# A two-layer RWKV-7/attention backbone on one core: running decays by a sum of exponents, token mixing in one VectorE pass, both heads' removal keys in one instruction

## The chip, the cores and the metric

The kernel runs on one core of one Trainium2 chip. The metric is device microseconds of one execution. The engines are named as the profile names them: PE (TensorE matmul) with PEld (its weight loads), DVE (VectorE), ACT (ScalarE), POOL (GpSimd) and SP (SyncE, which issues most DMAs). Each engine works through its own list of instructions in order; semaphores tie the lists together.

## The reference

Two layers work on a context stream and a latent stream of 256 tokens each, width 1024. A layer makes one modulated input, projects it with one weight matrix `w_in`, and feeds three mixers: latent attention, a short convolution, and a bidirectional recurrence. Their outputs are gated, merged and projected, and a SwiGLU feed-forward follows. The change lies in the recurrence alone. Cut to what it touches:

```python
def rwkv_features(part, mu, ...):
    up = _pad_seq(part)
    part = part + (0.5 * (up[:, :-2] + up[:, 2:]) - part) * mu         # token mixing
    r, k, v, wd, ad, gd = _split(part, ...)
    w_log = -softplus(-(w0 + tanh(wd) @ w_up)) - 0.5
    decay = exp(-exp(w_log))                                            # per token and channel
    a = sigmoid(a0 + ad @ a_up)
    kk = k * k_k / norm_per_head                                        # removal key
    k_dir = k * (1 + (a - 1) * k_a)

def step(S, inp):                                                       # once forward, once backward
    r, w, k, v, kk, a = inp
    S = S * w - (S @ kk) (kk * a)^T + v k^T
    return S, S @ r
```

With `exp(w_log) = sigmoid(x) * exp(-0.5)` and the sigmoid written as `0.5 + 0.5 tanh(x/2)`, one token's decay is `exp(-0.5 CEXP (tanh + 1))`, where `CEXP = exp(-0.5)`. The kernel runs the recurrence in chunks of 64 tokens. A chunk needs the product `P` of the decays from the chunk's start to each token, and its inverse `Pi`.

## The kernel before

Products of weights and activations run as three float32r matmuls (`mm3`, L199 to L201): every piece of weights is fetched by SP, copied to its high part on ACT (L188) and its low part formed on DVE or, for every third or fifth piece, on POOL (L189). These products take most of PE's time.

In the recurrence, `feature` (L424) takes each of 15 column tiles of the projection: ACT copies it out of PSUM with a zero at either end (`pp`, L429), POOL adds the two neighbours (`nb`, L432), and DVE finishes the mixing in two passes (L433: half the sum minus the token; L435: times `mu`, plus the token). The result goes to DRAM.

`rwkv_half` (L897) is called for each layer and each stream, four times in all. It handles eight units, each a pair of heads `hp` and a direction `z`. `stage1` prepares a unit: the removal key `kk` (L936, once for both directions), the low-rank products on PE (L957), two tanh on ACT (L959, L962), the decay `tw` and its inverse `di` as two exponentials (L965, L966), two POOL copies of the decays at the chunk starts into `first` and `firsti` (tiles `fd` and `fi`, L967, L968), and two running products on DVE (L971, L972), started afresh at each chunk by max and min. `stage2` builds `FM`: its removal part on DVE, one instruction of 64 partitions for each head (L987), its key part on POOL (L990); then `AR` on DVE and POOL, the chunk products on PE (L1006), and their masked copies (`LB`, `AR`) on ACT and DVE. `stage1` of the next unit is written ahead of `stage2` of the present one.

The four calls stand in three stretches of the run: layer 0's first stream about 120 to 215 us, layer 0's second about 340 to 390 us, layer 1's both about 1235 to 1430 us. Between and behind them PE works through the columns of `w_in` that the recurrence does not need (compressed queries and keys, gates, convolution), and pieces of these products also stand among the recurrence's own matmuls in PE's list.

The order on every engine is set when the program is built, by a scheduler that lists instructions by its own costs; it isn't written by hand. A change of an instruction can therefore move others.

Of the kernel before, what the change touches and what calls it, by code (L numbers as in the profile page):

```python
# [32 lines left out]
# columns of the packed per-channel vectors  # L33
# [24 lines left out]
# columns of the output that DVE finishes  # L58
# [16 lines left out]
def body(ctx: ExitStack, tc: tile.TileContext, A: dict, out: bass.AP, dbg=None, upto=None):  # L75
# [39 lines left out]
    # ---------------------------------------------------------------- constants  # L115
# [10 lines left out]
    ebias = ct("ebias", [128, 2])  # L126
# [12 lines left out]
    pool.memset(ebias[:, 0:1], -0.5 * CEXP)  # L139
    pool.memset(ebias[:, 1:2], 0.5 * CEXP)  # L140
# [6 lines left out]
    for l in range(NL):  # L147
        w0 = VOFF["rw_w0"]
        dve.tensor_scalar(out=hv[l][:, 0:16], in0=sv[:, l, w0:w0 + 16], scalar1=0.5, scalar2=None, op0=ALU.mult)
        ka = VOFF["rw_k_a"]  # L150
        dve.tensor_scalar(out=hv[l][:, 16:20], in0=sv[:, l, ka:ka + 4], scalar1=0.5, scalar2=None, op0=ALU.mult)
        dve.tensor_scalar(out=hv[l][:, 20:24], in0=sv[:, l, ka:ka + 4], scalar1=-0.5, scalar2=1.0, op0=ALU.mult,
                          op1=ALU.add)

    # ---------------------------------------------------------------- DRAM scratch
# [47 lines left out]
    def split(src, hi, lo, scale=None):  # L203
        """hi + lo = src * scale"""
# [18 lines left out]
    def mod_out(ps, n):  # L223
        """rows of partial sums of n slots -> columns [128, slot, stream] without their bias"""
# [9 lines left out]
    def mod_rows(l, i, bank=None):  # L234
        """vector i as rows in DRAM, for the token-major gate"""
# [34 lines left out]
    def to_fm(src, tt, h, xf, dst):  # L270
        """half of the columns, token-major -> modulated, transposed, split"""
# [25 lines left out]
    # ---------------------------------------------------------------- layer norm (token-major) of alpha x + g o  # L297
# [5 lines left out]
    def residual(z, acc, gz, xr, stg):  # L303
        """z = alpha x + g o and its mean, variance and inverse deviation per token"""
# [13 lines left out]
    def post(l, sub, accs, stg, dst, res_in, res_out):  # L318
        """accs[tt] = two banks of o; a function of tt: residual, norm, and what the next sub-layer needs"""
# [20 lines left out]
        def end(tt):  # L340
            """the output's tokens: by halves of the columns, on every engine"""
# [6 lines left out]
            # (z - mean) rs g + b  # L348
# [37 lines left out]
    # ---------------------------------------------------------------- mixers: one 128-column tile of w_in  # L386
# [960 lines left out]
```

## Time and profile before

| | us |
|---|---|
| median of 3 runs | 1935.84 (1932.49 to 1936.29) |
| span of the profiled execution, which has no other time of its own | 1933.0 |
| PE busy | 1843.0 (95%) |
| DVE busy | 1189.0 (62%) |
| ACT busy | 813.9 (42%) |
| POOL busy | 518.9 (27%) |

The profile is of one execution. A group's row gives line, engine, operation, tiles and shape, the count, then busy time and the mean of one in ns, then the engine's idle time just before such instructions with what ended it. The granted clock (PEclk) is TensorE's, as a share of its full 2.4 GHz; a stretch at 0.82 spent part of its time at the lower level, 1.2 GHz. In rows of waits the figures are the total in us, how often, and the longest.

### The profile page before, as it was taken

To read this page: it belongs to the slowest core of one execution; us is meant where nothing else is said; L and a number is where in the kernel's file an instruction comes from. 1 tells how busy PE (TensorE), PEld (TensorE's weight loads), DVE (VectorE), ACT (ScalarE), POOL (GpSimd) and SP (SyncE) were. 2 spreads that over 40 slices of the span, in tenths; PEclk is the share of its full clock that TensorE was granted. 3 is DMA by queue.
4 is the path that set the end of the run, shared out by engine and by line. 5 is a ranking of instruction groups with operands and counts; after the bars stand their busy time and mean duration, and the time that the engine had idled before them with its cause. 6 is when DMAs were issued, how large, how long until landed. Compare 5 with 4: busy or idle time off the path is not lost. (4 is left out here: it accounts for less than half of the span.)

```text
span 1933.0 us, 35208 instructions
## 1 busy us (share of the span) xinstructions
PE 1843.0 (95%) x13556; PEld 1507.4 (78%) x13556; DVE 1189.0 (62%) x2202; ACT 813.9 (42%) x1736; POOL 518.9 (27%) x614
## 2 busy tenths in 40 slices
PE   7999999999989999999999998999998999979998
PEld 5877777777767767877888887777787896869996
DVE  4578724974457778633333356598978358875665
ACT  2356333534235443333333223465553355535552
POOL 1467113611124223200000016465522133320001
PEclk9998999899989999999999998987899999989999
DMA  8443444244485427433334324453356474566563
GB/s 329 133 142 112 148 130 134 88 137 129 148 284 196 126 62 243 153 131 131 99 98 142 120 87 156 128 145 118 100 180 192 159 257 138 155 232 228 184 231 118
DMA packets 150728, 300.72 MB, mean 156 GB/s; under 512 B 30433, under 2 KB 85793, under 8 KB 150561
## 3 DMA queue, kind: packets, MB, share of 16 engines
q1 hardware_dynamic: 147584, 289.88, 45.9%
q10 hardware_dynamic: 2976, 8.59, 1.3%
q8 instruction: 107, 1.75, 0.4%
q14 instruction: 61, 0.49, 0.1%
HBM read 261.69 MB, written 36.73 MB: 154 GB/s over the span
## 5 line engine op out<-in xcount | busy, mean ns | idle before, releaser
L188 ACT CAST hi<-raw 128x512 fp32r<-128x512 f32 x548 | 331.4, 617 | 553.5 <-PE pg L200 138.7
L189 DVE TENSOR_TENSOR lo<-raw,hi 128x512 fp32r<-128x512 f32 x454 | 331.8, 737 | 371.4 <-ACT hi L188 353.0
L199 PE MATMUL pg<-xh,hi 128*128 128x512 f32 (+1 forms) x912 | 341.3, 376 | 3.5 <-ACT pp L429 2.5
L200 PE MATMUL pg<-xl,hi 128*128 128x512 f32 (+1 forms) x912 | 335.4, 368 | 0.5 <-DVE xl L207 0.5
L201 PE MATMUL pg<-xh,lo 128*128 128x512 f32 (+1 forms) x912 | 334.3, 367 | 0.0
L201 PE MATMUL p_f<-x2h,lo 128*128 128x256 f32 (+1 forms) x688 | 231.9, 337 | 2.2 <-DVE lo L189 2.2
L199 PE MATMUL p_f<-x2h,hi 128*128 128x256 f32 (+1 forms) x688 | 232.7, 338 | 1.0 <-ACT hi L188 1.0
L200 PE MATMUL p_f<-x2l,hi 128*128 128x256 f32 (+1 forms) x688 | 231.6, 337 | 0.6 <-DVE x2l L207 0.6
L189 POOL TENSOR_TENSOR lo<-raw,hi 128x512 fp32r<-128x512 f32 x94 | 126.2, 1343 | 379.5 <-ACT hi L188 345.2
L199 PEld LDWEIGHTS pg<-xh,hi 128*128 128x128 f32 x912 | 183.8, 202 | 35.5 <-issue 6.3
L200 PEld LDWEIGHTS pg<-xl,hi 128*128 128x128 f32 x912 | 184.1, 202 | 26.3 <-issue 3.2
L201 PEld LDWEIGHTS pg<-xh,lo 128*128 128x128 f32 x912 | 183.8, 202 | 23.6 <-issue 1.1
L295 POOL TENSOR_TENSOR rs<-rs,mhalf 128x1 f32<-128x1 f32 x12 | 9.1, 760 | 580.0 <-DVE rs L314 580.0
L199 PEld LDWEIGHTS p_f<-x2h,hi 128*128 128x128 f32 x688 | 131.5, 191 | 16.0 <-ACT hi L188 2.9
L201 PEld LDWEIGHTS p_f<-x2h,lo 128*128 128x128 f32 x688 | 131.4, 191 | 15.8 <-DVE lo L189 2.5
L200 PEld LDWEIGHTS p_f<-x2l,hi 128*128 128x128 f32 x688 | 131.5, 191 | 13.8 <-DVE x2l L207 0.9
L1006 PE MATMUL p_G<-AR,FM 64*128 64x128 f32 x384 | 54.1, 298 | 7.5 <-POOL lo L189 2.4
L613 POOL TENSOR_TENSOR acc<-acc,gts 128x512 f32<-128x512 f32 (+1 forms) x32 | 38.9, 1224 | 82.7 <-DVE gts L611 71.2
L1006 PEld LDWEIGHTS p_G<-AR,FM 64*128 64x128 f32 x384 | 46.8, 200 | 17.9 <-issue 7.6
L990 POOL TENSOR_TENSOR FM<-ta,di 64x256 f32<-64x256 f32 x64 | 53.9, 842 | 23.7 <-PE p_G L1018 15.7
L220 PE MATMUL pg<-raw,cs 128*32 128x128 f32 x1024 | 56.0, 308 | 2.8 <-DMA raw<-in_modw_dram 1.5
L283 ACT ACTIVATE xf<-p_f,modB,modA 128x128 f32<-128x128 f32 x40 | 17.4, 457 | 85.8 <-PE p_f L276 61.2
(391 smaller groups left out, 3678.5 us busy)
## 6 DMA issues: line engine op xcount, KB each, us to landing
raw<-in_win_dram SPq DMA_DIRECT2D x114, 512.0 KB, 4.4
raw<-in_modw_dram SPq DMA_DIRECT2D x96, 512.0 KB, 4.1
raw<-in_w_dram SPq DMA_DIRECT2D x88, 512.0 KB, 3.6
raw<-in_ffn_w_dram SPq DMA_DIRECT2D x44, 512.0 KB, 4.2
raw<-in_wo_dram SPq DMA_DIRECT2D x24, 512.0 KB, 3.5
raw<-in_w_out_dram SPq DMA_DIRECT2D x16, 512.0 KB, 3.6
feat<-nb SPq DMA_DIRECT2D x25, 256.0 KB, 2.6
gate<-gt SPq DMA_DIRECT2D x24, 256.0 KB, 2.8
```

The lines of the kernel that those rows point to most:

```text
L188: act.copy(out=hi, in_=r)
L189: e.tensor_tensor(out=lo, in0=r, in1=hi.bitcast(F32), op=ALU.subtract)
L199: pe.matmul(ps, wh, xh, start=first, stop=False, skip_group_check=True)
L200: pe.matmul(ps, wh, xl, start=False, stop=False, skip_group_check=True)
L201: pe.matmul(ps, wl, xh, start=False, stop=last, skip_group_check=True)
L220: pe.matmul(ps[32 * (k % 4):32 * (k % 4) + 32, 0:128], cs[:, o:o + 32], raw[:, k], start=(j == 0 and k < 4), stop=(k >= 4), skip_group_che ...
L283: act.activation(out=xf[:, kk], in_=pt[:, k * 128:(k + 1) * 128], func=ACTF.Identity, scale=modA[:, kk, z:z + 1], bias=modB[:, kk, z:z + 1])
L295: pool.tensor_tensor(out=out_, in0=in_, in1=e, op=ALU.pow)
L613: pool.tensor_tensor(out=a, in0=a, in1=g, op=ALU.add)
L990: pool.tensor_tensor(out=FM[r, :, k0:k0 + 64], in0=rc(ta[r]), in1=rc(Pi[r]), op=ALU.mult)
L1006: pe.matmul(ps[:, j * 128:j * 128 + ncol], FM[r, j], AR[z][r, e, hp, j, 0:ncol], start=True, stop=True)
```

## The change

Decays. One token's exponent is a constant times `tanh + 1`, so the running product is the exponential of a running sum. POOL adds 1 to the tanh, one DVE scan sums it within the chunk (the constant tile `again` is 0 where a chunk starts, 1 elsewhere), and two exponentials on ACT make `Pi` and `P` from the sum. The second scan, the two POOL copies for each unit and the tile `fi` go.

Mixing. `mu` is halved and `1 - mu` prepared at the start. ACT scales the token in place, and one DVE pass adds half of `mu` times the neighbours' sum.

Removal keys. One DVE instruction over all 128 partitions writes the removal part of `FM` for both heads into columns 64 to 127; ACT copies the first head's half to columns 0 to 63, and POOL's key part of the first head then overwrites its columns 64 to 127, after that of the second head.

Other lines change only in comments, in line numbers, and in reading halved parameters from `sv` in place of `hv`.

```diff
@@ constants, run once @@
-        dve.tensor_scalar(out=hv[l][:, 0:16], in0=sv[:, l, w0:w0 + 16], scalar1=0.5, scalar2=None, op0=ALU.mult)
+        dve.tensor_scalar(out=sv[:, l, w0:w0 + 16], in0=sv[:, l, w0:w0 + 16], scalar1=0.5, scalar2=None, op0=ALU.mult)
...
+        dve.tensor_scalar(out=hv[l][:, 4:19], in0=sv[:, l, mu:mu + 15], scalar1=-1.0, scalar2=1.0, op0=ALU.mult,
                           op1=ALU.add)
+        dve.tensor_scalar(out=sv[:, l, mu:mu + 15], in0=sv[:, l, mu:mu + 15], scalar1=0.5, scalar2=None, op0=ALU.mult)
@@ feature @@
                 pool.tensor_tensor(out=n_, in0=pp[:, a:2, 0:HT], in1=pp[:, a:2, 2:HT + 2], op=ALU.add)
-                dve.scalar_tensor_tensor(out=n_, in0=n_, scalar=0.5, in1=pp[:, a:2, 1:HT + 1], op0=ALU.mult,
-                                         op1=ALU.subtract)
+                act.mul(out=pp[:, a:2, 1:HT + 1], in_=pp[:, a:2, 1:HT + 1], mul=hv[l][:, 4 + m:5 + m])
                 dve.scalar_tensor_tensor(out=n_, in0=n_, scalar=col(l, "rw_mu", m), in1=pp[:, a:2, 1:HT + 1],
                                          op0=ALU.mult, op1=ALU.add)
@@ rwkv_half @@
-        first = rt("fd", [128, HT])             # decay where a chunk starts, else 0
-        firsti = rt("fi", [128, HT])            # its inverse there, else out of reach
-        pool.memset(first, 0.0)
-        pool.memset(firsti, 3.0e38)
+        again = rt("fd", [128, HT])
+        pool.memset(again, 1.0)
+        pool.memset(again[:, 0:HT:C], 0.0)
@@ stage1 @@
+            pool.tensor_scalar(out=tw, in0=tw, scalar1=1.0, scalar2=None, op0=ALU.add)
+            dve.tensor_tensor_scan(out=tw, data0=again, data1=tw, initial=0.0, op0=ALU.mult, op1=ALU.add)
             di = rt("di", [128, HT], bufs=2)
-            act.activation(out=di, in_=tw, func=ACTF.Exp, scale=0.5 * CEXP, bias=ebias[:, 1:2])
-            act.activation(out=tw, in_=tw, func=ACTF.Exp, scale=-0.5 * CEXP, bias=ebias[:, 0:1])
-            pool.tensor_copy(out=first[:, 0:HT:C], in_=tw[:, 0:HT:C])
-            pool.tensor_copy(out=firsti[:, 0:HT:C], in_=di[:, 0:HT:C])
             P, Pi = tw, di
-            dve.tensor_tensor_scan(out=P, data0=tw, data1=first, initial=1.0, op0=ALU.mult, op1=ALU.max)
-            dve.tensor_tensor_scan(out=Pi, data0=di, data1=firsti, initial=1.0, op0=ALU.mult, op1=ALU.min)
+            act.activation(out=Pi, in_=tw, func=ACTF.Exp, scale=0.5 * CEXP)
+            act.activation(out=P, in_=tw, func=ACTF.Exp, scale=-0.5 * CEXP)
@@ stage2 @@
-            for e in range(2):
+            dve.scalar_tensor_tensor(out=FM[:, :, 64:128], in0=v4(bp), scalar=0.5, in1=v4(Pi), op0=ALU.mult, op1=ALU.mult)
+            act.copy(out=FM[0:64, :, 0:64], in_=FM[0:64, :, 64:128])
+            for e in (1, 0):
...
-                dve.scalar_tensor_tensor(out=FM[r, :, b0:b0 + 64], in0=v4(bp[r]), scalar=0.5, in1=v4(Pi[r]),
-                                         op0=ALU.mult, op1=ALU.mult)
```

The change also moves instructions. DVE's list in layer 0's second stream, around the third unit's removal keys, before (a scan is listed as SCALAR_TENSOR_TENSOR; `di` and `tw` are the two running products, `bp` half of the removal key):

```order
L936 SCALAR_TENSOR_TENSOR kk<-kf,sv,p_c_2669 128x256
L975 SCALAR_TENSOR_TENSOR bp<-ta,kk 128x256
L972 SCALAR_TENSOR_TENSOR di<-di,fi 128x256
L987 SCALAR_TENSOR_TENSOR FM<-bp,di 64x4x64 x2
L1012 TENSOR_TENSOR LB<-p_G,mask 64x4x64
L1014 TENSOR_TENSOR AR_2563<-p_G,mask 64x512
L971 SCALAR_TENSOR_TENSOR tw<-tw,fd 128x256
```

And the same place now (L935 is the removal key, L972 `bp`, L965 the one scan, L981 the removal keys of both heads):

```order
L935 SCALAR_TENSOR_TENSOR kk<-kf,sv,p_c_2647 128x256
L972 SCALAR_TENSOR_TENSOR bp<-ta,kk 128x256
L965 SCALAR_TENSOR_TENSOR tw<-fd,tw 128x256
L981 SCALAR_TENSOR_TENSOR FM<-bp,di 128x4x64
L990 TENSOR_TENSOR AR_2545<-kk,tw 64x4x63 x2
L1010 TENSOR_TENSOR LB<-p_G,mask 64x4x64
```

Before, the removal keys followed their scan on DVE itself; now an exponential on ACT stands between the scan and the removal keys, and DVE's list has nothing between the two here. At most one row stands between them in 8 of the 32 units: seven in layer 0, one in layer 1.

ACT's list at the same stream's second unit, before (`hi` are pieces of weights, `gt` a gate):

```order
L959 ACTIVATE tw<-p_c_2609,hv_84 128x256
L962 ACTIVATE ta<-p_c_2609,hv_84 128x256
L944 CAST uhl<-lw 128x256
L965 ACTIVATE di<-tw,ebias 128x256
L976 ACTIVATE ta<-ta,hv_84 128x256
L966 ACTIVATE tw<-tw,ebias 128x256
L188 CAST hi<-raw 128x512 x2
L537 ACTIVATE gt<-pg 128x2x256
```

And now (L968 and L969 are the two exponentials of the sum, L973 the former L976, L982 the copy of the first head's removal keys):

```order
L958 ACTIVATE tw<-p_c_2589,sv 128x256
L961 ACTIVATE ta<-p_c_2589,sv 128x256
L943 CAST uhl<-lw 128x256
L973 ACTIVATE ta<-ta,hv_83,sv 128x256
L968 ACTIVATE di<-tw 128x256
L969 ACTIVATE tw<-tw 128x256
L982 COPY FM<-FM 64x4x64
L189 CAST hi<-raw 128x512 x2
L537 ACTIVATE gt<-pg 128x2x256
```

The two exponentials moved behind a wait for DVE's scan, the copy behind a wait for DVE's removal keys, and the weights' copies and the gate stand behind them all. PE's list keeps its contents, and nearly its order.

## Rows read from the trace of the kernel before

**Rows 1.** The page: PE's busy time, and the granted clock in 40 slices.
```profile
PE 1843.0 (95%) x13556; PEld 1507.4 (78%) x13556; DVE 1189.0 (62%) x2202; ACT 813.9 (42%) x1736; POOL 518.9 (27%) x614
...
PEclk9998999899989999999999998987899999989999
```

**Rows 2.** Windows: length; busy (count) of PE, PEld, DVE, ACT, POOL; clock; DMA, GB/s.
```profile
57.00:120.00 63.00, 62.35 (x291) 50.93 (x291) 37.95 (x49) 25.98 (x46) 38.68 (x50) 1.00 0.51 159
120.00:215.00 95.00, 88.89 (x490) 70.90 (x489) 78.90 (x138) 53.43 (x136) 52.36 (x76) 0.87 0.37 113
...
340.00:390.00 50.00, 47.33 (x278) 35.53 (x276) 44.22 (x72) 29.06 (x77) 32.79 (x50) 0.86 0.26 82
...
1235.00:1430.00 195.00, 180.82 (x1228) 151.66 (x1226) 165.24 (x289) 113.66 (x278) 97.81 (x149) 0.82 0.43 130
```

**Rows 3.** Waits of PE in 120 to 215 us: total, times, longest.
```profile
PE pg L521 <- ACT sqs L518: 2.3, 1, 2.3
PE p_G L1006 <- ACT cqs L514: 2.1, 1, 2.1
PE p_G L1006 <- ACT vou L452: 1.1, 1, 1.1
```

**Rows 4.** Waits of PE in 340 to 390 us.
```profile
PE p_c L199 <- DVE kk L936: 2.7, 1, 2.7
```

**Rows 5.** Waits of PE in 1235 to 1430 us.
```profile
PE p_u L957 <- DVE kk L936: 6.9, 4, 3.9
PE p_G L1006 <- POOL lo L189: 2.4, 1, 2.4
PE pg L199 <- ACT pp L429: 1.6, 1, 1.6
PE p_G L1006 <- DVE iv L1044: 1.6, 1, 1.6
```

**Rows 6.** Timeline of PE, its two longest waits: start, length, instruction, [wait].
```profile
1304.74 1.22 PE L957 MATMUL p_u<-twd,lw 64*128 64x256 f32 x2 [2.36 <-DVE kk L936]
...
1344.38 1.22 PE L957 MATMUL p_u<-twd,lw 64*128 64x256 f32 x2 [3.87 <-DVE kk L936]
```

**Rows 7.** Timeline of DVE ahead of the wait that ended at 1344 us.
```profile
1330.21 1.40 DVE L987 SCALAR_TENSOR_TENSOR FM<-bp,di 64x256 f32<-64x256 f32 x2
...
1333.02 0.68 DVE L972 TENSOR_TENSOR_SCAN di<-di,fi 128x256 f32<-128x256 f32 x1
...
1339.39 1.21 DVE L972 TENSOR_TENSOR_SCAN di<-di,fi 128x256 f32<-128x256 f32 x1
...
1344.67 0.41 DVE L987 SCALAR_TENSOR_TENSOR FM<-bp,di 64x256 f32<-64x256 f32 x1
```

**Rows 8.** Timeline of DVE ahead of the wait that ended at 1304 us.
```profile
1298.20 0.41 DVE L433 SCALAR_TENSOR_TENSOR nb<-nb,pp 128x256 f32<-128x256 f32 x1
...
1300.18 1.21 DVE L972 TENSOR_TENSOR_SCAN di<-di,fi 128x256 f32<-128x256 f32 x1
1301.31 1.31 DVE L987 SCALAR_TENSOR_TENSOR FM<-bp,di 64x256 f32<-64x256 f32 x2
```

**Rows 9.** Groups of ACT nearest to what is added: count, busy us, mean ns, idle.
```profile
L1008 ACT COPY LB<-p_G 32x256 f32<-32x256 f32 x48 | 17.2, 359 | 22.6 <-PE p_G L1006 22.2
L965 ACT ACTIVATE di<-tw,ebias 128x256 f32<-128x256 f32 x32 | 16.4, 512 | 1.3 <-DVE FM L987 1.2
```

**Rows 10.** Groups of POOL: nearest to what is added, and the copies removed.
```profile
L978 POOL TENSOR_TENSOR ta<-ta,kf 128x256 f32<-128x256 f32 x32 | 26.0, 813 | 14.9 <-ACT ta L976 14.2
L967 POOL COPY fd<-tw 128x4 f32<-128x4 f32 x32 | 11.1, 347 | 5.2 <-ACT tw L966 4.9
L968 POOL COPY fi<-di 128x4 f32<-128x4 f32 x32 | 8.9, 278 | 21.8 <-ACT di L965 21.3
L1114 POOL COPY SV<-S 64x256 f32<-64x256 f32 x16 | 8.6, 539 | 0.7
```

**Rows 11.** Waits of ACT over the whole run, one row.
```profile
ACT ta L976 <- DVE bp L975: 21.2, 16, 3.2
```

More of the change, by code (lines that the diff above doesn't have):

```diff
@@ L125, in body @@
     pick = ct("pick", [128, 8])
-    ebias = ct("ebias", [128, 2])
     ssq = ct("ssq", [128, 5, 4])
@@ L138, in body @@
     pool.memset(cs, 0.0)
-    pool.memset(ebias[:, 0:1], -0.5 * CEXP)
-    pool.memset(ebias[:, 1:2], 0.5 * CEXP)
     act.activation(out=cs[:, CP:].rearrange("p (k c) -> p k c", c=32)[:, :, 0:2], in_=cvec, func=ACTF.Silu)
@@ L148, in body @@
         w0 = VOFF["rw_w0"]
-        dve.tensor_scalar(out=hv[l][:, 0:16], in0=sv[:, l, w0:w0 + 16], scalar1=0.5, scalar2=None, op0=ALU.mult)
+        dve.tensor_scalar(out=sv[:, l, w0:w0 + 16], in0=sv[:, l, w0:w0 + 16], scalar1=0.5, scalar2=None, op0=ALU.mult)
         ka = VOFF["rw_k_a"]
-        dve.tensor_scalar(out=hv[l][:, 16:20], in0=sv[:, l, ka:ka + 4], scalar1=0.5, scalar2=None, op0=ALU.mult)
-        dve.tensor_scalar(out=hv[l][:, 20:24], in0=sv[:, l, ka:ka + 4], scalar1=-0.5, scalar2=1.0, op0=ALU.mult,
+        dve.tensor_scalar(out=hv[l][:, 0:4], in0=sv[:, l, ka:ka + 4], scalar1=-0.5, scalar2=1.0, op0=ALU.mult,
                           op1=ALU.add)
+        dve.tensor_scalar(out=sv[:, l, ka:ka + 4], in0=sv[:, l, ka:ka + 4], scalar1=0.5, scalar2=None, op0=ALU.mult)
+        mu = VOFF["rw_mu"]
+        dve.tensor_scalar(out=hv[l][:, 4:19], in0=sv[:, l, mu:mu + 15], scalar1=-1.0, scalar2=1.0, op0=ALU.mult,
+                          op1=ALU.add)
+        dve.tensor_scalar(out=sv[:, l, mu:mu + 15], in0=sv[:, l, mu:mu + 15], scalar1=0.5, scalar2=None, op0=ALU.mult)
     def dt_(name, shape):
@@ L462, in layer @@
             for n, w, bufs in (("kf", HT, 2), ("kk", HT, 2), ("rr", HT, 2), ("tw", HT, 2), ("ta", HT, 2), ("di", HT, 2),
-                               ("bp", HT, 2), ("FM", 512, 2), ("fd", HT, 1), ("fi", HT, 1),
+                               ("bp", HT, 2), ("FM", 512, 2), ("fd", HT, 1),
                                ("lw", HT, 1 if U3[l] else 2), ("iv", 256, 1)) + ((("tms", 512, 2),) if last else (("pad", 2560, 1),)):
@@ L959, in stage1 @@
             act.activation(out=tw, in_=rv(pu[:, 0:HT]), func=ACTF.Tanh, scale=0.5,
[L960 removed]
+                           bias=col(l, "rw_w0", 4 * z + hp))
             ta = rt("ta", [128, HT], bufs=2)
             act.activation(out=ta, in_=rv(pu[:, HT:T]), func=ACTF.Tanh, scale=0.5,
[L963 removed]
+                           bias=col(l, "rw_a0", 4 * z + hp))
+            pool.tensor_scalar(out=tw, in0=tw, scalar1=1.0, scalar2=None, op0=ALU.add)
+            dve.tensor_tensor_scan(out=tw, data0=again, data1=tw, initial=0.0, op0=ALU.mult, op1=ALU.add)
             di = rt("di", [128, HT], bufs=2)
[L965 to L968 removed]
             P, Pi = tw, di
[L971 to L972 removed]
+            act.activation(out=Pi, in_=tw, func=ACTF.Exp, scale=0.5 * CEXP)
+            act.activation(out=P, in_=tw, func=ACTF.Exp, scale=-0.5 * CEXP)
             pool.tensor_copy(out=PC[:, z, :, hp], in_=P[:, C - 1:HT:C])
@@ L975, in stage1 @@
             dve.scalar_tensor_tensor(out=bp, in0=ta, scalar=1.0, in1=rv(kk), op0=ALU.add, op1=ALU.mult)
-            act.activation(out=ta, in_=ta, func=ACTF.Identity, scale=hv[l][:, 16 + hp:17 + hp],
-                           bias=hv[l][:, 20 + hp:21 + hp])
+            act.activation(out=ta, in_=ta, func=ACTF.Identity, scale=col(l, "rw_k_a", hp),
+                           bias=hv[l][:, hp:hp + 1])
             pool.tensor_tensor(out=ta, in0=ta, in1=rv(kf), op=ALU.mult)
@@ L982, in stage2 @@
             FM = rt("FM", [128, 4, 128], bufs=2)
-            for e in range(2):
+            dve.scalar_tensor_tensor(out=FM[:, :, 64:128], in0=v4(bp), scalar=0.5, in1=v4(Pi), op0=ALU.mult, op1=ALU.mult)
+            act.copy(out=FM[0:64, :, 0:64], in_=FM[0:64, :, 64:128])
+            for e in (1, 0):
                 r = slice(64 * e, 64 * e + 64)
-                b0, k0 = (0, 64) if e == 0 else (64, 0)
+                k0 = 64 - 64 * e
                 P4 = v4(P[r])
-                dve.scalar_tensor_tensor(out=FM[r, :, b0:b0 + 64], in0=v4(bp[r]), scalar=0.5, in1=v4(Pi[r]),
-                                         op0=ALU.mult, op1=ALU.mult)
                 rc = (lambda a: v4(a)) if z == 0 else (lambda a: v4(a)[:, :, ::-1])
```

2 lines of the change are left out of this document (removed).

## The prediction

> **What bounds the kernel now.** First the page's busy shares [rows 1]: PE is busy 95% of the span, no other engine above 62%. The change takes nothing from PE, so it can only give back time in which PE idles or runs slowly. The page's clock digits say where to look: most slices read 9, the low ones (8, once 7) lie mainly in the first third and around two thirds of the span. I then read windows over the recurrence [rows 2]. From 57 to 120 us, where most of layer 0's mixing is done, PE is busy 62.35 of 63 us at clock 1.00: DVE work removed there buys nothing. The three stretches with units are different:
>
> - 120 to 215 us: idle 95 - 88.89 = 6.1; low clock 0.13 x 95 = 12.4
> - 340 to 390 us: idle 50 - 47.33 = 2.7; low clock 0.14 x 50 = 7.0
> - 1235 to 1430 us: idle 195 - 180.82 = 14.2; low clock 0.18 x 195 = 35.1
>
> A stretch at granted clock 0.82 has spent part of its time at 1.2 instead of 2.4 GHz; the missing share times the length is what it would win at full clock (it counts idle time at the lower level twice, an error I accept). Together 23.0 us of idle and 54.5 us of low clock: 77.4 us is all that this change can reach. In these stretches DVE is the busiest engine after PE: 78.90 + 44.22 + 165.24 = 288 us of 340, or 85%. ACT has 196 us, 58%.
>
> Last the waits of PE in each stretch [rows 3 to 5]. DVE ended 2.7 + 6.9 + 1.6 = 11.2 us of the 23.0 (49%), ACT 2.3 + 2.1 + 1.1 + 1.6 = 7.1 (31%), POOL 2.4; the remainder is in waits too short to list. PE's slow time comes beside such holes, so I share the low clock out in the same proportion, which is an assumption: 0.49 x 77.4 = 37.9 us hang on DVE, 0.31 x 77.4 = 24.0 us on ACT. The long waits are all for `kk` (L936). That instruction needs little itself; it is late because DVE's list ahead of it is full.
>
> **What goes.** For each of 32 units DVE loses one scan and one of two 64-partition products of `FM`. Undisturbed, the scan takes 0.68 and the product 0.41 us [rows 7]: 32 x 1.09 = 34.9 us, and a product over 128 partitions with as many elements in each should cost no more than the one that stays. Thirty mixing passes go too, most of them under full PE; a few stand in the stretches. How much of the waits for `kk` goes with them is read from DVE's list ahead of the two longest [rows 6 to 8]. Ahead of the 3.87 us wait, one `FM` product (0.41) and two scans L972 (0.68 each) vanish: 1.77. Ahead of the 2.36 us wait, a mixing pass (0.41), a scan (0.68) and a product (0.41): 1.50. That is 3.27 of 6.23 us, 52%. I take 52% of the 37.9 us that hang on DVE: 19.9.
>
> The trace shows these instructions also at greater length: the scan at 1.21, pairs of products at 1.40 and 1.31 for two [rows 7, 8]. By those durations 2.59 + 2.28 = 4.87 of 6.23 us would vanish, 78%. A reason to refuse the greater numbers is in the Trainium skill, page "SBUF — State Buffer", section "Who interferes with whom": a VectorE instruction with two SBUF inputs contends with a GpSimd instruction that reads SBUF, and whichever comes second is blocked outright. The two durations of one shape agree with it. By that rule the excess is waiting and falls on the next such DVE instruction, and the removal is worth 52%; without it the gain below would be 19.4 instead of 10.9 us, and the time 1916.
>
> **What comes in.** ACT gets 32 copies of half of `FM`. No row shows just this copy; the nearest are 0.36 (32 partitions, as many elements in each) and 0.51 us for an activation of the same width [rows 9], so 11.5 to 16.4 us, and I take 11.5, a copy being a copy. Some eight of the 30 mixing multiplications fall into the stretches (layer 1's late tiles have one stream, so 256 elements: 0.51 each, 4.1). The others lie where PE is full, and cost nothing while ACT keeps up (25.98 of 63 us [rows 2]). POOL gives up 64 short copies, 11.1 + 8.9 = 20.0 us, and gets 32 additions over 128x256: between the one-input copy's 0.539 and the two-input product's 0.813 [rows 10], 17.2 to 26.0 us, so -2.8 to +6.0; with one input I take the lower end and count nothing. The small setup instructions run while the first weights come.
>
> More important are the waits that are added. The exponentials now stand behind the sum, so each unit goes POOL, DVE, ACT, DVE, ACT where it went ACT, POOL, DVE. On ACT the weights' copies and the gates are queued behind the blocked exponentials and the blocked copy; PE waits for both. On DVE everything to the next `kk` is queued behind `FM`. The instruction order shows the sum and `FM` at most one row apart in eight units; in the others DVE has work between. At 0.51 us for the exponential between them [rows 9] that is 4.1 us of blocked DVE, and as much on ACT. Both ends: nothing, if other instructions always cover it; or for all 32 units what ACT waits today when it stands behind DVE for `bp`, 21.2 / 16 = 1.3 us each [rows 11], 42 us.
>
> **The sum.** DVE: 4.1 of 34.9 us removed are given back, 12%, so 0.88 x 19.9 = 17.5 us gained. ACT: 196 + 11.5 + 4.1 + 4.1 = 216 of 340 us. I let the loss that hangs on ACT grow as busy over free time, from 196/144 = 1.36 to 216/124 = 1.74, by 28%: 0.28 x 24.0 = 6.6 us lost. Net 10.9 us: 1933.0 - 10.9 = 1922.1 for the span. The profiled span is 2.8 us under the median of the runs, 1935.84, so 1925 us. PE's list keeps its contents and almost its order, so what PE saves in these stretches is not taken back behind them.
>
> **Rivals.**
>
> - The new hop decides (slower). The place is ACT's list in the units, the price the 1.3 us for each unit above. ACT: 196 + 15.6 + 42 = 254 of 340, busy over free 2.96, so its loss grows 2.17 times, +28 us. DVE stands 32 x 0.51 = 16.3 us behind the exponentials, so its gain falls by 47% to 10.5. Net +17.6: 1953 us. It decides from about 0.7 us a unit: there ACT loses 14.9 and DVE gains 14.9. For it: layer 0's second stream, where six of the eight adjacent pairs lie, is the densest in units. Against: ACT is free 42% of these stretches.
> - The gain is hidden anyway (no change). Three of the listed causes are not DVE's, and a shorter wait for `kk` may only uncover POOL's low parts (2.4) or ACT's copies: 1933 to 1939 us, 1936 in the middle. For it: 31% of the idle time is ACT's, in the first stretch all that is listed.
> - All that hangs on DVE goes and ACT costs nothing: 1933.0 - 37.9 + 2.8 = 1898 us. For it: waits behind a queue fall faster than the work in it; DVE at 85% would be at 75%. Against: today's two long waits are only half made of removed work.
> - The change could fail to relieve DVE at all, if the scan with a constant operand or the 128-partition product ran longer than those before. Then DVE's mean durations would show it; I fold this into the slower case.
>
> **How the numbers follow.** Forecast 0.42, full relief 0.18, no change 0.17, slower 0.23. A measurement of this kernel can tell about 0.2%, 4 us, from no change. Faster 0.42 + 0.18 = 0.60, same 0.17, slower 0.23. The range leaves out half of the full relief's chance below and somewhat under half of the slower case's above: 1905 to 1946. The forecast's own range is 1916 to 1931, since the relief may be 78% or, with ACT's waits doubled, some 5 us.
>
> **What would show it.** Right: in the three stretches DVE's busy time falls from 288 to about 250 us; the waits of PE for `kk` fall from 9.6 to about 5 us; the clock in the last stretch rises from 0.82 towards 0.86; DVE shows idle time before `FM` ended by the exponential, under 10 us in all; POOL's busy time is as before; outside the stretches nothing moves by more than a few us. Wrong: ACT's waits for the scan sum to more than 20 us, with PE waiting for gates and weights; or the waits for `kk` stay although DVE is less busy; or the scheduler's new order costs or gives time in attention or the feed-forward, where the change has no part.

## The result, and the profile after

| | before | after |
|---|---|---|
| median, us | 1936.07 (4 runs) | 1916.2 (4 runs, 1910.53 to 1922.2) |
| ratio | 1 | 0.9894, 95% interval 0.9861 to 0.9927 |
| profiled execution, span | 1933.0 | 1914.8 (time 1916.59) |
| PE busy | 1843.0 | 1822.1 |
| DVE / ACT / POOL busy | 1189.0 / 813.9 / 518.9 | 1125.5 / 835.3 / 530.1 |

The change makes the kernel about 20 us faster, against a forecast of 1925 us, 10.9 us faster. A second measurement of it (experiment 5) gave 0.9915 (0.9884 to 0.9946), 16 us; both intervals hold 0.990. The direction and the range were right, the size was too small. Below it turns out that the gain in the stretches with units was priced too low, and that losses outside them, priced at nothing, took part of it back.

The page of the changed kernel: PE's line and the granted clock, to be held against [rows 1].

```profile
PE 1822.1 (95%) x13556; PEld 1492.2 (78%) x13556; DVE 1125.5 (59%) x2112; ACT 835.3 (44%) x1798; POOL 530.1 (28%) x580
...
PEclk9999999999989999999999998878899999979999
```

PE does the same 13556 matmuls in 20.9 us less busy time; its idle time is 92.7 us against 90.0. So the gain is the clock's: matmuls ran longer before because more of them ran at the lower level. The runs without a profile say the same: over all 86 runs of the kernel before in the experiments the mean clock is 0.957 and the mean time 1938.6 us; over 20 runs of the changed kernel and of two variants of it that do the same work it is 0.966 and 1917.9. Clock times time is 1855 and 1853.

Windows of the changed kernel over the stretches of [rows 2], moved forward by 5 us from the second stream on, by 8 at layer 1's units and by 15 behind them (columns as there). The last two lie behind the recurrence of layer 1.

```profile
57.00:120.00 63.00, 60.65 (x278) 49.65 (x277) 25.88 (x34) 32.62 (x57) 34.32 (x48) 0.97 0.49 160
120.00:215.00 95.00, 92.96 (x547) 74.21 (x546) 72.35 (x125) 58.74 (x151) 58.64 (x70) 0.95 0.40 124
335.00:385.00 50.00, 50.00 (x355) 38.63 (x355) 40.52 (x66) 34.28 (x92) 37.44 (x47) 1.00 0.31 103
1227.00:1415.00 188.00, 173.45 (x1379) 147.04 (x1378) 146.94 (x267) 119.63 (x301) 103.07 (x133) 0.85 0.45 139
1415.00:1585.00 170.00, 160.27 (x2070) 140.88 (x2069) 103.14 (x212) 75.91 (x164) 48.41 (x49) 1.00 0.62 195
1585.00:1745.00 160.00, 143.13 (x1043) 120.89 (x1043) 117.26 (x239) 72.05 (x160) 44.04 (x38) 0.93 0.57 185
```

The same two last stretches of the kernel before, which were not shown:

```profile
1430.00:1600.00 170.00, 163.82 (x2209) 144.45 (x2208) 105.20 (x219) 75.47 (x161) 45.21 (x49) 0.99 0.60 195
1600.00:1760.00 160.00, 143.67 (x1058) 119.80 (x1059) 121.19 (x247) 74.67 (x166) 45.73 (x41) 0.95 0.58 190
```

Idle time plus missing clock share times length, as in the prediction:

| stretch (before) | before | after | difference |
|---|---|---|---|
| 57 to 120, mixing of layer 0 | 0.7 | 4.2 | +3.6 |
| 120 to 215, units, layer 0 | 18.5 | 6.8 | -11.7 |
| 340 to 390, units, layer 0 | 9.7 | 0 | -9.7 |
| 1235 to 1430, units, layer 1 | 49.3 | 42.8 | -6.5 |
| 1430 to 1760, behind them | 32.2 | 37.8 | +5.6 |

The three stretches with units won 27.9 us, of which idle time makes 6.4 (23.0 to 16.6) and the clock the remainder. Elsewhere 9.2 us were given back. The sum, -18.7, lies near the difference of the spans, 18.2; the stretches that are left out differ by 1 to 2 us.

Since the order changed, a window does not hold the same work on both sides (278 matmuls in the third stretch before, 355 after). A surer measure is one matmul that both kernels reach with the same work done. From 740 to 1160 us, between the units of layer 0 and those of layer 1, PE's order is the same in both; here is one product there, before and after (start, length, instruction):

```profile
1143.97 0.39 PE L199 MATMUL p_f<-hi,hh 128*128 128x512 f32 x1
```

```profile
1126.58 0.39 PE L200 MATMUL p_f<-hi,hh 128*128 128x512 f32 x1
```

It comes 17.4 us earlier, and the span ends 18.2 us earlier. So nearly the whole gain of this pair of profiles is made in layer 0, and layer 1 adds some 0.8 us: what its units won (6.5) was given back behind them (5.6). In a second profile of the changed kernel layer 0's part repeats (PE 92.96 and 93.00 us at clock 0.95 in 120 to 215, a full 65.00 at 1.00 in 335 to 400 in both), while layer 1's units had clock 0.80 instead of 0.86 in 1240 to 1420. The product above comes at 1126.04 there, 17.9 us earlier than before, but that execution ended only 5.3 us earlier. So one profile says little about layer 1.

Waits of PE in the changed kernel from 120 to 215 us, against [rows 3]. From 335 to 385 us there is none, against [rows 4].

```profile
PE p_G L1004 <- DVE AR L1012: 1.0, 2, 0.6
PE pg L521 <- ACT sqs L518: 0.7, 1, 0.7
PE p_y L1016 <- ACT TM L1018: 0.3, 1, 0.3
```

And from 1227 to 1415 us, against [rows 5].

```profile
PE p_G L1004 <- DVE AR L1012: 4.5, 3, 2.4
PE p_u L956 <- DVE kk L935: 4.3, 2, 2.8
PE p_G L1016 <- DVE AR L1012: 3.5, 3, 1.9
```

The waits for `kk` fell from 9.6 to 4.3 us, and a new one took part of their place: 8.0 us for `AR` (L1012, the masked copy of the chunk products), which is the next thing on DVE that PE needs. In layer 1's stretch all waits that DVE ended even rose, from 8.5 to 13.1 us. In the first stretch the waits that ACT ended shrank from 5.5 to 1.0 us.

What the work costs now. DVE over the whole run, before and then after (columns as in [rows 9]):

```profile
L987 DVE SCALAR_TENSOR_TENSOR FM<-bp,di 64x256 f32<-64x256 f32 x64 | 46.3, 723 | 5.1 <-PE p_G L1018 4.1
...
L971 DVE TENSOR_TENSOR_SCAN tw<-tw,fd 128x256 f32<-128x256 f32 x32 | 26.2, 818 | 0.5
L972 DVE TENSOR_TENSOR_SCAN di<-di,fi 128x256 f32<-128x256 f32 x32 | 25.4, 794 | 6.1 <-POOL fi L968 5.7
```

```profile
L965 DVE TENSOR_TENSOR_SCAN tw<-fd,tw 128x256 f32<-128x256 f32 x32 | 32.0, 1003 | 9.4 <-POOL tw L964 8.6 <-POOL pp L429 0.7
...
L981 DVE SCALAR_TENSOR_TENSOR FM<-bp,di 128x256 f32<-128x256 f32 x32 | 18.9, 591 | 9.9 <-PE p_G L1016 6.5 <-ACT di L968 3.2
```

Scans went from 51.6 to 32.0 us, removal keys from 46.3 to 18.9: 47.0 us less, not 34.9. ACT and POOL, the added and the shortened instructions:

```profile
L968 ACT ACTIVATE di<-tw 128x256 f32<-128x256 f32 x32 | 13.2, 414 | 18.2 <-DVE tw L965 18.1
L982 ACT COPY FM<-FM 64x256 f32<-64x256 f32 x32 | 12.8, 401 | 10.2 <-DVE FM L981 10.1
```

```profile
L964 POOL TENSOR_SCALAR tw<-tw 128x256 f32<-128x256 f32 x32 | 29.7, 929 | 10.4 <-ACT tw L958 9.8
```

ACT now waits 18.1 + 10.1 us for the sum and for `FM`; in exchange its waits for `bp`, 21.2 us in [rows 11], fell to 9.4:

```profile
ACT ta L973 <- DVE bp L972: 9.4, 11, 2.6
```

### The profile page after: what moved, and what is told of

It is laid out like the page before. It is cut to its first block, busy times and chain, and to the rows that moved or that the text cites. A ratio compares the mean times of both kernels' runs of the same rounds, so it can differ in the third digit from the quotient of the medians.

```text
span 1914.8 us, 35130 instructions
## 1 busy us (share of the span) xinstructions
PE 1822.1 (95%) x13556; PEld 1492.2 (78%) x13556; DVE 1125.5 (59%) x2112; ACT 835.3 (44%) x1798; POOL 530.1 (28%) x580
## 3 DMA queue, kind: packets, MB, share of 16 engines
q1 hardware_dynamic: 147584, 289.88, 46.3%
## 5 line engine op out<-in xcount | busy, mean ns | idle before, releaser
L200 PE MATMUL pg<-xh,hi 128*128 128x512 f32 (+1 forms) x912 | 336.8, 371 | 7.5 <-DVE u L548 2.1
L201 PE MATMUL pg<-xl,hi 128*128 128x512 f32 (+1 forms) x912 | 331.5, 364 | 1.3 <-DVE xl L208 1.3
L1163 POOL TENSOR_TENSOR S<-S,PC 128x256 f32<-128x256 f32 x28 | 19.1, 681 | 148.1 <-DVE SV L1162 133.2
L1044 DVE TENSOR_TENSOR sq<-sq,iv 128x31 f32<-128x31 f32 (+15 forms) x124 | 53.6, 432 | 3.0
L221 PE MATMUL pg<-raw,cs 128*32 128x128 f32 x1024 | 51.1, 301 | 3.3 <-DMA raw<-in_modw_dram 3.2
```

The lines of the kernel that those rows point to most:

```text
L200: pe.matmul(ps, wh, xh, start=first, stop=False, skip_group_check=True)
L201: pe.matmul(ps, wh, xl, start=False, stop=False, skip_group_check=True)
L221: pe.matmul(ps[32 * (k % 4):32 * (k % 4) + 32, 0:128], cs[:, o:o + 32], raw[:, k], start=(j == 0 and k < 4), stop=(k >= 4), skip_group_che ...
L1044: dve.tensor_tensor(out=Ti[:, j + 1:32, 0:w], in0=Ti[:, j + 1:32, 0:w], in1=tv, op=ALU.subtract)
L1163: pool.tensor_tensor(out=S[z], in0=S[z], in1=pc, op=ALU.mult)
```

## The experiments

Every experiment was timed in five rounds beside the kernel before, whose median was 1938 to 1939 us there. The ratio is to the kernel before, with its 95% interval, some 0.2 to 0.4% to either side. It is not the quotient of the medians, from which it differs by up to some 0.2% (experiment 3: 0.9994, medians 1.0015). Five theories are told apart. Q: the gain comes from DVE's list of work in the units, which has become shorter. O: the scheduler draws a new order at every edit, and the gain is luck of that draw. A: ACT has gained (shorter exponentials, fewer waits). M: the dropped tile `fi` moved what lies behind it in SBUF. H: what the removal keys' part takes from DVE it gives back by its hop to ACT.

| run | median | ratio | interval |
|---|---|---|---|
| changed kernel, first measurement | 1916.2 | 0.9894 | 0.9861 to 0.9927 |
| 5 changed kernel, again | 1922.0 | 0.9915 | 0.9884 to 0.9946 |
| 6 its order redrawn | 1915.7 | 0.9885 | 0.9855 to 0.9916 |
| 9 room of `fi` kept | 1916.5 | 0.9887 | 0.9860 to 0.9914 |
| 1 sum alone | 1922.6 | 0.9910 | 0.9888 to 0.9932 |
| 12 products on POOL | 1920.3 | 0.9895 | 0.9857 to 0.9932 |
| 10 second scan back, in place | 1930.9 | 0.9964 | 0.9939 to 0.9989 |
| 11 keys undone | 1934.0 | 0.9964 | 0.9946 to 0.9983 |
| 3 keys alone | 1942.2 | 0.9994 | 0.9971 to 1.0016 |
| 8 second scan back, into a scratch tile | 1938.6 | 1.0005 | 0.9987 to 1.0023 |
| 2 mixing alone | 1945.0 | 1.0028 | 1.0008 to 1.0048 |
| 4 all DVE work back | 1945.6 | 1.0030 | 1.0012 to 1.0048 |
| 7 kernel before, order redrawn | 1941.8 | 1.0032 | 1.0011 to 1.0054 |

### 1. The sum alone

```diff
 # kernel before
...
+            pool.tensor_scalar(out=tw, in0=tw, scalar1=1.0, scalar2=None, op0=ALU.add)
+            dve.tensor_tensor_scan(out=tw, data0=again, data1=tw, initial=0.0, op0=ALU.mult, op1=ALU.add)
-            act.activation(out=di, in_=tw, func=ACTF.Exp, scale=0.5 * CEXP, bias=ebias[:, 1:2])
...
-            dve.tensor_tensor_scan(out=Pi, data0=di, data1=firsti, initial=1.0, op0=ALU.mult, op1=ALU.min)
+            act.activation(out=Pi, in_=tw, func=ACTF.Exp, scale=0.5 * CEXP)
+            act.activation(out=P, in_=tw, func=ACTF.Exp, scale=-0.5 * CEXP)
```

> The kernel before with the decays' part alone: one running sum on DVE in place of two running products, the addition on POOL, no small copies; mixing and removal keys as before. DVE loses 32 x 0.68 = 21.8 of the 34.9 us that the whole change takes from the units. Theory Q (the gain of 20 us is DVE's list in the unit stretches becoming shorter): 21.8/34.9 = 62% of it, 12 us, 1924 us (1920 to 1928). Theory O (the gain is luck of the instruction order, which every edit reshuffles): nothing follows from the work, anything from 1916 to 1942. Theory A (the gain is ACT's: two shorter exponentials without a bias tile, 64 x 0.09 = 6 us, and the end of its waits for the removal key bp): all of it, 1916 us or less, since the copies and multiplications that burden ACT are absent here.

Measured: 17 us faster (13 to 22), nearly the whole gain, more than the 12 that Q gave it but inside its 1920 to 1928. It speaks against one half of A: ACT's waits for `bp` did not end, they rose from 21.2 to 27.6 us in this run's profile. The shorter exponentials are left to A.

### 2. The mixing alone

```diff
 # kernel before
...
-                dve.scalar_tensor_tensor(out=n_, in0=n_, scalar=0.5, in1=pp[:, a:2, 1:HT + 1], op0=ALU.mult,
-                                         op1=ALU.subtract)
+                act.mul(out=pp[:, a:2, 1:HT + 1], in_=pp[:, a:2, 1:HT + 1], mul=hv[l][:, 24 + m:25 + m])
```

> The kernel before with the mixing part alone: one DVE pass and one ACT multiplication in place of two DVE passes. Theory Q: only some eight of 30 passes lie in unit stretches, 8 x 0.41 = 3.3 us of DVE, so 0 to 2 us faster: 1934 to 1936 us. Theory O: anything within some 8 us on either side, 1928 to 1944. Theory A: ACT gets 4 us more in the stretches, 1936 to 1940.

Measured: 5.4 us slower (1.6 to 9.3), against Q's 0 to 2 us faster. The place is 57 to 120 us. Windows of this stretch, first of the sum alone (experiment 1, old mixing), then of this run:

```profile
57.00:120.00 63.00, 62.43 (x291) 51.04 (x290) 36.26 (x48) 25.91 (x46) 39.24 (x51) 1.00 0.50 165
```

```profile
57.00:120.00 63.00, 59.96 (x275) 49.42 (x274) 20.99 (x33) 30.23 (x52) 33.83 (x46) 0.97 0.48 158
```

PE loses 2.5 us and part of its clock here, and gets 16 matmuls fewer done. It is not this run's accident: in the four kernels with the old mixing PE is busy 62.35 to 62.55 us of this stretch at clock 1.00, in all ten with the new one 57.76 to 61.43 us at 0.95 to 0.97. What makes the holes differs. In this run it is one hole of 3.04 us, for ACT's `kn` (L878), which stood in ACT's list behind a multiplication (L437) that waited for POOL, and then waited for a DMA itself. Timeline of ACT, then of PE (start, length, instruction, wait):

```profile
84.05 0.72 ACT L437 ACTIVATE pp<-pp,hv 128x512 f32<-128x512 f32 x1 [1.91 <-POOL nb L436]
85.47 0.72 ACT L878 ACTIVATE kn<-kn,sv 128x512 f32<-128x512 f32 x1 [0.70 <-DMA kn<-feat]
```

```profile
86.25 1.10 PE L886 MATMUL p_y<-bones,kn 128*128 128x2 f32 x8 [3.04 <-ACT kn L878]
```

In the changed kernel there are two. Timeline of PE:

```profile
90.11 0.39 PE L200 MATMUL pg<-xh,hi 128*128 128x512 f32 x1
92.04 1.02 PE L883 MATMUL p_y<-bones,kn 128*128 128x2 f32 x8 [1.54 <-DVE rn L886]
92.93 0.48 PE L201 MATMUL pg<-xl,hi 128*128 128x512 f32 x1
93.24 0.40 PE L202 MATMUL pg<-xh,lo 128*128 128x512 f32 x1
94.45 0.80 PE L200 MATMUL pg<-xh,hi 128*128 128x512 f32 x1 [0.81 <-ACT pp L430]
95.04 0.63 PE L201 MATMUL pg<-xl,hi 128*128 128x512 f32 x1
```

PE idled 1.54 us and 0.81 us; from the second hole on a matmul of the same shape takes 0.63 instead of 0.39 us. That hole is for ACT's copy of a feature out of PSUM (L430). The copy had waited 1.31 us for POOL, which cleared the ends of `pp` (L429) only behind a product of the first unit that waited for a DMA:

```profile
92.21 1.52 POOL L994 TENSOR_TENSOR AR<-rr,tw 64x256 f32<-64x256 f32 x2 [2.88 <-DMA rr<-feat]
93.68 0.10 POOL L429 MEMSET pp<- 128x4 f32 x1
```

ACT's list has no mixing multiplication between 84 and 94 us. So the multiplication itself does not make these two holes; they come with the order that the change brought. Over the run DVE's mixing pass now waits 30.7 us for ACT's multiplication, where the first of its two passes waited 20.0 us for POOL. Whether the longer chain or the new order costs PE its time is not told apart; that it does, all ten profiles show.

### 3. The removal keys alone

```diff
-            for e in range(2):
+            dve.scalar_tensor_tensor(out=FM[:, :, 64:128], in0=v4(bp), scalar=0.5, in1=v4(Pi), op0=ALU.mult, op1=ALU.mult)
+            act.copy(out=FM[0:64, :, 0:64], in_=FM[0:64, :, 64:128])
+            for e in (1, 0):
...
-                dve.scalar_tensor_tensor(out=FM[r, :, b0:b0 + 64], in0=v4(bp[r]), scalar=0.5, in1=v4(Pi[r]),
-                                         op0=ALU.mult, op1=ALU.mult)
```

> The kernel before with the removal keys' part alone: one DVE product over 128 partitions and one ACT copy in place of two products over 64. DVE loses 32 x 0.41 = 13.1 us, ACT gets 32 x 0.40 = 12.8. Theory Q: 13.1/34.9 = 38% of 20 us, 7.5 us, less what the hop to ACT costs: 1928 to 1933 us. Theory O: anything within some 8 us on either side. Theory A: only ACT's burden is left, slower, 1938 to 1944 us.

Measured: no change that can be seen, 1.2 us faster by the ratio with an interval from 5.6 faster to 3.1 slower, and 3 us slower by the medians. Less than Q said; A's small loss isn't excluded. Open until experiment 11.

### 4. All of DVE's removed work given back

```diff
 # changed kernel, plus
...
+            jk = rt("jk", [128, HT])
+            dve.tensor_tensor_scan(out=jk, data0=again, data1=again, initial=0.0, op0=ALU.mult, op1=ALU.add)
...
+            dve.scalar_tensor_tensor(out=v4(jk[0:64]), in0=v4(bp[0:64]), scalar=0.5, in1=v4(Pi[0:64]), op0=ALU.mult, op1=ALU.mult)
```

> The changed kernel, with the DVE work that it took from the units given back without any use: in each unit a second scan (of the constant tile, into a scratch tile) right behind the sum and a 64-partition product (into the same scratch tile) right behind FM; ACT, POOL and PE have the work of the changed kernel. DVE gets 32 x 1.09 = 34.9 us. Theory Q: the gain goes back nearly whole, 1930 to 1937 us. Theory A: DVE's load doesn't matter, 1914 to 1920. Theory O: the order is drawn anew, anything from 1910 to 1936, and the waits of PE for kk need not grow.

Measured: 5.8 us slower than the kernel before, so the gain is gone and more. A falls: ACT and POOL have the changed kernel's work here. Windows of the added instructions alone (columns: DVE busy and count, clock, DMA):

```profile
120.00:215.00 95.00, 12.28 (x16) 0.89 0.36 114
335.00:400.00 65.00, 10.45 (x14) 0.89 0.34 113
1227.00:1430.00 203.00, 22.72 (x30) 0.85 0.44 137
```

60 of the 64 lie in the stretches with units, where they take 45.5 us and DVE waits for them 1.3 us in the whole run; in layer 0 the clock is back at 0.89, from 0.95 and 1.00. But the edit also redraws the order and puts a tile where `fi` had been, so O and, a rival seen only later, M, are open.

### 5, 6 and 7. How much is order?

Experiment 5 is the changed kernel again. Experiments 6 and 7 are the changed kernel and the kernel before with one loop turned round:

```diff
 # products within the chunks, masked
-            for e in range(2):
+            for e in (1, 0):
                 r = slice(64 * e, 64 * e + 64)
                 o = slice(64 - 64 * e, 128 - 64 * e)
```

> The changed kernel as it is, once more, so that its gain is known as closely as that of the experiments. All theories: 0.986 to 0.993 of the kernel before, some 20 us faster.

> The changed kernel with the two heads' products within the chunks issued in the other order (head 1 first). The work is the same, instruction by instruction, but it moves the instructions of PE against each other about as much as the change itself did (PE's list agrees with the changed one to 0.84, the list before to 0.83). Theory Q (a shorter list on DVE): no change beyond 0.3%, 1914 to 1924 us on a chip where the kernel before takes 1939. Theory O (order by luck): anything from 1910 to 1945, the gain may be gone.

> The kernel before with the same edit: head 1's products first, the work the same. Theory Q: 1934 to 1944 us. Theory O: anything from 1915 to 1950. With the run above this gives the spread that order alone makes, against which the parts' results (17 us faster, 5 slower, none) have to be held.

Measured: 0.9915, 0.9885 and 1.0032. The redrawn changed kernel is as fast as the changed one, the redrawn kernel before 6 us slower than itself. Order is worth some 6 us at most in these two draws; the two families stay 16 us or more apart (0.9915 against 1). O falls as the cause of the gain, but it sets how finely single parts can be read: experiment 2's 5.4 us would not stand on the time alone, without the windows.

### 8. Only the second scan given back

```diff
 # changed kernel, plus
...
+            jk = rt("jk", [128, HT])
+            dve.tensor_tensor_scan(out=jk, data0=again, data1=again, initial=0.0, op0=ALU.mult, op1=ALU.add)
```

> The changed kernel with only the second scan given back to DVE in each unit (of the constant tile, into a scratch tile; its result is not used): 32 x 0.68 = 21.8 us of the 34.9 us of the earlier run that gave all back and lost 27 us. Theory Q: 62% of that loss, 17 us, so 1932 to 1938 us on a chip where the kernel before takes 1939. Theory A (ACT's shorter exponentials and fewer waits made the gain): 1917 to 1922. Theory O: no relation, 1912 to 1945.

Measured: no gain left, 1938.6 us, just above Q's 1932 to 1938. The profile warns against taking it so. Windows of the added scans alone (columns as in experiment 4):

```profile
57.00:120.00 63.00, 7.00 (x8) 0.95 0.46 147
120.00:215.00 95.00, 6.00 (x8) 0.95 0.40 122
335.00:400.00 65.00, 0.00 (x0) 1.00 0.37 119
1227.00:1415.00 188.00, 7.46 (x8) 0.84 0.42 129
```

The scans depend on nothing but a constant, so the scheduler was free to pull them forward: only half lie in units, and eight sit in the mixing stretch, where PE is busy 57.76 us, the lowest of all kernels. In 335 to 400 us, without an added scan, PE stays full at clock 1.00. The run shows that DVE work costs time, not that it does so in the units. It also made us look at what the slow kernels shared: a tile in `fi`'s place.

### 9 and 10. The tile without the work, and the work without the tile

```diff
 # 9: changed kernel
-                               ("bp", HT, 2), ("FM", 512, 2), ("fd", HT, 1),
+                               ("bp", HT, 2), ("FM", 512, 2), ("fd", HT, 1), ("jk", HT, 1),
```

```diff
 # 10: changed kernel
+            di = rt("di", [128, HT], bufs=2)
+            dve.tensor_tensor_scan(out=di, data0=again, data1=again, initial=0.0, op0=ALU.mult, op1=ALU.add)
             dve.tensor_tensor_scan(out=tw, data0=again, data1=tw, initial=0.0, op0=ALU.mult, op1=ALU.add)
-            di = rt("di", [128, HT], bufs=2)
```

> The changed kernel with the room of the dropped tile fi (256 columns) kept in the recurrence's pool and never used. Not one instruction is added and the order on every engine is the changed kernel's; only the tiles behind it in SBUF lie 1 KB a partition higher, as they do in the kernel before and in the runs that gave DVE work back. It is run because all kernels with that room took 1938 to 1946 us and all without it 1916 to 1923. Theory M (the gain is where the tiles lie, not the work): 1935 to 1943 us, the gain is gone. Theory Q (DVE's list in the units): no effect, 1916 to 1924.

> The changed kernel with the second scan given back to DVE without that room: in each unit a scan of the constant tile writes di just ahead of the sum, and the exponential writes over it. 32 x 0.68 = 21.8 us more on DVE in the units, and the tiles lie where they lie in the changed kernel. Theory Q: the gain is gone as with the scan given back into a scratch tile, 1932 to 1942 us. Theory M: little or nothing, 1916 to 1926 us.

Measured: 0.9887 and 0.9964. The tile alone costs nothing: M falls. The scan alone, tied to its unit by the tile it writes, costs 9 to 15 us of the gain's 16 to 22: 1930.9 us lies just under Q's 1932 to 1942 and outside M's 1916 to 1926. But it does not add work alone. The added scan writes a `di` that POOL still reads for an earlier unit, so DVE waits for POOL there, 8.9 us:

```profile
L966 DVE TENSOR_TENSOR_SCAN di<-fd 128x256 f32<-128x256 f32 x32 | 27.4, 861 | 9.4 <-POOL FM L989 8.9 <-POOL pp L429 0.5
```

How much of the 9 to 15 us is this wait is not known. With M gone, experiment 4 counts again, which has the work in the units without such a wait and lost 22 to 28 us, far more than order made in experiments 6 and 7. Q rests on experiments 4 and 10 together. Windows of 335 to 400 us, in the order changed kernel, tile only, scan back, each from its own trace:

```profile
335.00:400.00 65.00, 65.00 (x462) 50.12 (x462) 54.01 (x98) 37.94 (x100) 39.10 (x49) 1.00 0.38 124
```

```profile
335.00:400.00 65.00, 65.00 (x452) 50.14 (x451) 53.68 (x97) 38.52 (x105) 40.84 (x50) 1.00 0.38 123
```

```profile
335.00:400.00 65.00, 62.66 (x430) 46.83 (x428) 51.19 (x82) 40.45 (x108) 45.55 (x54) 0.97 0.30 102
```

With the scan back PE has holes again, its clock falls, and 32 matmuls fewer get done than in the changed kernel. DVE isn't even busier in this window; it gets fewer other things done (82 instructions against 98).

### 11. The keys undone

```diff
 # changed kernel, the lines of experiment 3 taken back
```

> The changed kernel with the removal keys' part alone undone: two DVE products over 64 partitions in place of one over 128 and an ACT copy; sum and mixing stay. DVE gets 32 x 0.41 = 13.1 us back, ACT loses 32 x 0.40 = 12.8. Theory Q by DVE's load alone: the load-only run lost 13 us to 21.8, so 13.1 us of load lose 8: 1924 to 1930 us on a chip where the kernel before takes 1938. Theory H (what the part takes from DVE it gives back by its hop to ACT, as the run of this part alone with its nothing would say): 1914 to 1923 us, no loss.

Measured: 1934.0 us, 0.9964: without this part 9 to 15 us of the gain are missing, as in experiment 10. H falls for the changed kernel; Q's 8 us is too little. Windows of layer 0's two stretches with units:

```profile
120.00:215.00 95.00, 91.36 (x428) 72.72 (x427) 66.49 (x111) 53.80 (x136) 51.81 (x68) 0.82 0.32 99
...
335.00:400.00 65.00, 62.55 (x447) 48.67 (x450) 56.07 (x91) 41.92 (x113) 48.71 (x61) 0.97 0.35 117
```

Most of the loss lies in the first, at clock 0.82 against 0.95. Alone the part gave 1 us (experiment 3), here 9 to 15. Taking the three parts as adding up (sum -17, mixing +6, keys -5 us) fits experiments 1, 2, 3, 11 and the whole change within some 4.5 us, which is what order and the intervals allow. So whether the parts help one another isn't settled; nor is why a scan is worth more than Q gave it alone (17 us) and the keys less.

### 12. A product moved to POOL

```diff
 # changed kernel
-                dve.tensor_tensor(out=al[:, :, 1:64], in0=v4(kkr[r])[:, :, 1:64], in1=P4[:, :, 0:63], op=ALU.mult)
+                (pool if e else dve).tensor_tensor(out=al[:, :, 1:64], in0=v4(kkr[r])[:, :, 1:64], in1=P4[:, :, 0:63], op=ALU.mult)
```

> The changed kernel with one of each unit's two products kk x P (odd heads, 64 partitions x 252) moved from DVE to POOL: 32 x 0.57 = 18 us less on DVE, some 32 x 0.8 = 26 us more on POOL, which is busy 103 of 188 us in the last stretch with units and would be at 116 to 118. Theory Q with POOL off the path: DVE's load decides, 0.6 us per us, 11 us faster than the changed kernel: 1905 to 1911 us. Rival: POOL's products stand in the units' chain (PE waits for FM and AR from POOL), and the slower instruction costs what the list saves: 1914 to 1926 us.

Measured: 0.9895, 1920.3 us, no better than the changed kernel. Q's 1905 to 1911 was missed. The group of the scan on DVE in this run:

```profile
L965 DVE TENSOR_TENSOR_SCAN tw<-fd,tw 128x256 f32<-128x256 f32 x32 | 34.8, 1088 | 10.9 <-POOL tw L964 10.5
```

DVE was relieved of 32 products, some 18 us, and is busy 1116.5 us against 1125.5, only 9.0 less: the others became longer (the scan 1088 against 1003 ns), and POOL has 18.8 us more. Work that only changed sides between these two engines was not worth moving here. So Q holds for work that DVE gets back, and this run does not extend it to less work than the changed kernel's.

## Why the prediction was right, and where its sum was wrong

**The place was right in layer 0.** The gain lies in stretches with units, and PE's clock there is its form; experiments 4 and 10 show that DVE's work in the units decides over it. Of the signs, the clock of the last stretch went from 0.82 to 0.85 (forecast 0.86), the waits for `kk` to 4.3 us (about 5), DVE's idle time before `FM` ended by the exponential is 3.2 us (under 10); DVE's busy time in the three stretches fell from 288 (of 340) to 260 us (of 333) only (about 250). But the 52% was read from two waits in layer 1, where the waits that DVE ended rose in all and where this pair of profiles has some 0.8 us of gain. That the result lies in the range is in this part luck.

**The DVE term was sized too small.** The step that failed is "I take 52%", with 1.09 us a unit. It took the shortest durations on record as the price of the removed work. For the products 0.41 is the price of an undisturbed one, but the mean of 64 was 0.723, and the 128-partition product that does two of them takes 0.591: 27.4 us went, not 13.1. With the scans' 19.6 that is 47.0 us. The reason for the choice was the rule of the Trainium skill, page "SBUF — State Buffer", section "Who interferes with whom", that of two contending instructions the second is blocked outright. From it the prediction concluded that the excess only moves to the next one. For the scans the trace agrees with the conclusion: the remaining scan grew from a mean of 0.81 to 1.00 us, so a unit saved 19.6 / 32 = 0.61 us, even less than the 0.68 that was taken. For the products it doesn't: 27.4 / 32 = 0.86 us a unit went, more than their mean. So neither the shortest nor the mean duration was the price of either; that the two means, 1.53 us a unit, come near the 1.47 that went is chance. At the forecast's own rate, 17.5 us for 34.9, 47.0 us are worth 23.6, an estimate. The rejected version of the sum, with 78%, gave 1916 us, near what was measured, but by way of an ACT term that was wrong as well.

**The ACT term had the wrong sign.** Forecast was 6.6 us lost. ACT's busy time in the stretches came out as expected (212.7 us of 333; the forecast's 216 of 340 hold 4.1 of waiting), and its waits for the sum, 18.1 us, came close to the 20 that the prediction named as a sign of trouble (with those for `FM` 28.2). Yet PE's waits that ACT ended went from 8.6 us, of which the prediction lists 7.1, to 1.6 in the three stretches, and there is none for weights. Sharing the loss out by which engine ended PE's waits did not hold, for ACT or for DVE. Why ACT's part went is open. ACT's waits for DVE's `bp` fell from 21.2 us [rows 11] to 9.4 in the changed kernel, but they don't follow the gain: with the sum alone, 17 us faster, they rose to 27.6, and with the keys alone, no faster, they fell to 10.7. ACT also got 64 x 0.09 us back that were not foreseen (below).

**"Cost nothing while ACT keeps up" was wrong.** The mixing under a full PE was priced at nothing. It costs 3.6 us in 57 to 120 us in the changed kernel, and appears in every profile with the new mixing (experiment 2). ACT did keep up on average, 32.62 of 63 us; what PE waited for was late because of the order of waits on ACT and POOL.

**"Not taken back behind them" was wrong in this profile**: 5.6 us are lost behind layer 1's units. Since layer 1 differs by more between two profiles of the changed kernel, this is not a finding about the change.

So for this profile -10.9 should have been about -28 in the stretches, +4 in the mixing and +6 behind layer 1's units; how the -28 divide between the DVE and the ACT term no run shows. The rivals "the new hop decides" and "the gain is hidden" are refuted by the time itself; full relief would have needed 1898 us. The fourth, that the new instructions run longer, is refuted by the shortest of each: 0.67 us for a scan (0.66 before) and 0.41 for a product over 128 partitions (0.39 over 64). Not tried: sum and keys without the mixing, which the fit above would put some 22 us below the kernel before, an estimate.

## What to carry to other kernels

Where a clock that drops after holes is the loss, give a change on the engine that makes the holes a range of prices: here one kind of removed instruction was worth less than its shortest duration and the other more than its mean. Don't share the loss out by the engine that ended each wait: when one wait goes, the next in line takes its place. Moving work under a full engine is not free by itself: look at what that engine needs next, and at what now stands ahead of it. When every edit redraws the schedule, time one edit that changes order alone and one that changes addresses alone before believing any part's few microseconds; and when work is given back as a test, look whether it brings a wait of its own.

## What the runs showed of the hardware

- An exponential over 128x256 takes 0.41 us without a bias tile (L968 above) and 0.51 us with one [rows 9]; 64 of them gave ACT 6 us back. The Trainium skill, page "ScalarE: Activation LUTs", section "What ACT_TABLE_LOAD costs", states that each pointer operand adds some 93 ns; these rows agree.
- POOL's addition of a constant over 128x256, one input, has a mean of 929 ns: above the two-input product's 813 and 867 ns before and after, not near the copy's 539 [rows 10]. The prediction's lower end was wrong. POOL is busy 11.2 us more; DVE waited 8.6 us for these additions, and PE's waits in the three stretches name none of POOL's instructions.
- The long durations of DVE's scans and removal-key products fall together with work on POOL. Those that took over 1.15 times the shortest of their kind all overlapped a POOL instruction: 17 scans and 40 products before, 15 and 15 after. Of the short ones 26 of 47 scans before met no POOL instruction at all. In experiment 12, with more of the work on POOL, the scan's mean rose from 1003 to 1088 ns. Overlap alone is not enough: 21 of the 47 short scans overlapped POOL too.
- Between runs of one kernel time follows the granted clock: 23 runs of the kernel before, side by side, went from 1923.69 us at 0.969 to 1946.29 at 0.953.
